# Squares of three row blocks on VectorE instead of ScalarE, and one row scaling in two pieces, in a single-core encoder layer

## The chip, the cores and the metric

The kernel runs on one core of a Trainium2 chip. The metric is the device time of one execution in microseconds. Each core has TensorE (matrix multiplications, here PE, its weight loads PEld), VectorE (DVE), ScalarE (ACT), GpSimd (POOL) and SyncE (SP), each with an instruction queue of its own that is worked off in order; here SyncE's queue issues the DMA transfers that move tiles between DRAM and the on-chip memories SBUF and PSUM.

## The reference

One layer of a bidirectional encoder over two sequences of 256 and 2048 tokens, each with the same 16 learned meta tokens in front, d_model = 1024. All arrays are float32. Cut to what matters:

```python
def hybrid_layer(z, norm_w, w_in, q_norm_w, k_norm_w, sink, conv_w, conv_b, ln_w, ln_b, w_out):
    h = rmsnorm(z, norm_w)                       # z * rsqrt(mean(z*z) + 1e-6) * norm_w, per token
    proj = jnp.einsum('bld,de->ble', h, w_in)    # 1024 -> 2816
    q, k, v, g_att, c_val, c_glu, g_conv = jnp.split(proj, SPLIT_IDX, axis=-1)
    q = rmsnorm(q.reshape(B, L, N_HEADS, HEAD_DIM), q_norm_w)
    k = rmsnorm(k.reshape(B, L, N_KV_HEADS, HEAD_DIM), k_norm_w)
    v = v.reshape(B, L, N_KV_HEADS, HEAD_DIM)
    att = windowed_gqa(q, k, v, sink).reshape(B, L, W_ATT) * jax.nn.silu(g_att)
    cnv = conformer_conv(c_val, c_glu, conv_w, conv_b, ln_w, ln_b) * jax.nn.silu(g_conv)
    mixed = jnp.concatenate([att, cnv], axis=-1)
    return z + jnp.einsum('ble,ed->bld', mixed, w_out)
```

The change is in the first line, the normalization: for each token the sum of the squares of its 1024 values, and the scaling by the inverse root of their mean.

## The kernel before

The 2320 tokens (16 meta tokens and 18 blocks of 128) are the columns of the input projection. They are cut into six groups: group 0 of 400 columns (the meta tokens and blocks 1 to 3 of the rows, in the code `SEGS0`), and groups 1 to 5 of 384 columns, three blocks each. Two chunks of three groups go through the projection, `CHUNKS`; a chunk goes through eleven units of 256 output columns of `w_in`, and an item is one unit for one group. A projected unit is accumulated in PSUM from 24 matmuls per half: each float32 operand is split into a high part `xh` (or `ws` high) in the fp32r format and the rest, `xl`, and for each of the eight slices of 128 input features three products are summed, high by high, high by `xl`, and low weight by `xh` (`proj_et`, matmuls at L831).

A row block is loaded by `stats(i)` from `z` into a tile `xn` (L693). The function that it returns, `rest`, sums the squares (L700, on ScalarE, with an accumulator) into `ssq`, and GpSimd computes 1/rms in two instructions, at L128 and L129, into column `i` of `rstd`. Index 0 is the meta tokens, 1 to 3 are the other blocks of group 0, 4 to 6 group 1, 7 to 9 group 2. Blocks 0 to 3 have tiles of their own and write their squares to a spare tile `sq0`; block 4 has a tile of another pool, blocks from 5 on share the two buffers of the tag `xn`, and their squares are written over the block. So the load of block 7 goes into the buffer of block 5, the load of 8 into that of 6, the load of 9 into that of 7.

Group 0 is normalized by rows: VectorE multiplies each block by its 1/rms (L1102), TensorE transposes it in eight pieces of 128 columns (`turn0`, L1074; six right away, two later), and `split0` makes `xh` on ScalarE (L1082) and `xl` on VectorE (L1084). In front of the transposes of each block stand some warm-up matmuls (`busy`, L1067; each float32 one is two instructions in the trace). The two first weight units are split by ScalarE (L806) and VectorE (L807); for the second of them VectorE and GpSimd take turns. The groups from 1 on are loaded already transposed (`zt`, L717). TensorE spreads the three columns of `rstd` over partitions by three transposes into `bc` (`Prep.first`, L729), VectorE scales (`Prep.scale`, L745), ScalarE casts to `xh` (L762), VectorE and GpSimd take turns at `xl` (`Prep.split`, L771). The first item's results are gated: a sigmoid on ScalarE gives `sg` (L874), for which another activation table is loaded, and VectorE multiplies into `us` (L886). The convolution on VectorE (L914) comes later, as do attention and output projection.

The program is written in an order of ticks (`later(k, f)` puts work off by k ticks). On each engine a scheduler then sets the order when the program is built, by a simulated timeline (the context is opened with `schedule_with_timeline_sim=True`): what is ready goes first, and among ready instructions that which was written first. An instruction wrapped in `pinned`, `tc.keep_in_program_order`, stays behind everything that was written ahead of it for its engine. Pinned here are the squares of blocks 0 to 6 and the splits of the first two weight units, the row scalings of group 0, the warm-ups and the first six transposes. The squares of blocks 7 to 9 and the transposes into `bc` are not. At the start of item 0 the second weight unit is split, and behind it the squares of group 1 are written; `Prep.first` of group 1 comes one tick into item 1, the loads of blocks 7 to 9 with it and their squares a tick later; `Prep.first` of group 2 comes one tick into item 2.

Of the kernel before, what the change touches and what calls it, by code (L numbers as in the profile page):

```python
# [14 lines left out]
AF = mybir.ActivationFunctionType  # L15
ALU = mybir.AluOpType
# [3 lines left out]
D = 1024  # L20
# [59 lines left out]
def hymba_kernel(  # L80
# [11 lines left out]
    nc = tc.nc  # L92
# [31 lines left out]
    rstd = const.tile([P, NB + 1], F32, name="rstd")  # L124

    def rsqrt(dst, src, scale, eps):
        n = src.shape[-1]
        nc.gpsimd.tensor_scalar(src, src, scale, eps, op0=ALU.mult, op1=ALU.add)  # L128
        nc.gpsimd.tensor_tensor(dst, src, half[: src.shape[0], 0:n], op=ALU.pow)  # L129
# [545 lines left out]
    if True:  # L675
        rows0 = {}
        sq0 = yp.tile([P, YW], F32, tag="y", name="sq0")

        def pinned(op, yes=True):
            if yes:  # L680
                tc.keep_in_program_order(op)

        def stats(i):
            rows = NM if i == 0 else P
            r0 = 0 if i == 0 else NM + P * (i - 1)
            if i < 4:
                xn = cp.tile([P, UWID], F32, tag="us", name=f"xn{i}")[:, :D]
                rows0[i] = xn
            elif i == 4:
                xn = yp.tile([P, YW], F32, tag="y", name=f"xn{i}")[:, :D]  # L690
            else:
                xn = sp.tile([P, D], F32, tag="xn", name=f"xn{i}")
            dma = nc.sync.dma_start(xn[:rows], z[r0 : r0 + rows, :])  # L693
            if i >= PIN_X:
                tc.keep_in_program_order(dma)

            def rest():
                ssq = sp.tile([P, 1], F32, tag="ssq", name=f"ssq{i}", bufs=4)
                sq = sq0[:, :D] if i < 4 else xn
                pinned(nc.scalar.activation(sq[:rows], xn[:rows], AF.Square, accum_out=ssq[:rows]), i < 7)  # L700
                rsqrt(rstd[:rows, i : i + 1], ssq[:rows], 1.0 / D, EPS)

            return rest
# [360 lines left out]
        def busy(pt, n):  # L1064

            for _ in range(n):
                tc.keep_in_program_order(nc.tensor.matmul(pt[:, :P], ident, ident, start=True, stop=True))  # L1067

        def turn0(i, d):

            o, rows = SEGS0[i]
            if d not in cols0:
                cols0[d] = psum.tile([P, 512], F32, tag="cdcdabcd"[d], name=f"xt0_{d}")
            return nc.tensor.transpose(  # L1074
                cols0[d][:, o : o + rows], rows0[i][:rows, P * d : P * d + P], ident[:rows, :rows]
            )
# [22 lines left out]
        for i in range(4):  # L1099
            r[i]()  # L1100
            o, rows = SEGS0[i]
            pinned(nc.vector.tensor_scalar(rows0[i][:rows], rows0[i][:rows], rstd[:rows, i : i + 1], None, op0=ALU.mult))  # L1102
            busy(warmup, (10, 5, 2, 3)[i])
            for d in range(6):
                tc.keep_in_program_order(turn0(i, d))
# [176 lines left out]
```

## Time and profile before

| what | value |
|---|---|
| median of three runs | 959.06 us (958.97 to 959.19) |
| profiled execution, its own time | 959.35 us |
| span of its trace | 957.6 us |
| TensorE busy | 948.4 us, 99% |
| VectorE busy | 754.3 us, 79% |
| ScalarE busy | 423.1 us, 44% |
| GpSimd busy | 334.7 us, 35% |
| DMA, mean over the span | 178 GB/s |

Busy times are sums over the instructions of an engine in the profiled execution; TensorE's ends are modelled, and its warm-up matmuls count as busy too. Times in the rows are in microseconds from the start of the span, unless marked ns. In a row of the timeline the first number is the start, the second the time from the start of the first to the end of the last of the xN instructions merged in it, and in brackets stands how long the engine had been idle and what ended that.

### The profile page before, as it was taken

The page shows a single profiled execution, that of the slowest core. Times are in us where ns is not written, and L with a number is a line of the kernel's source. Part 1 is how long each engine was busy: PE and PEld are TensorE (multiplying, and loading weights), DVE is VectorE, ACT ScalarE, POOL GpSimd, SP SyncE. Part 2 cuts the span into 40 slices and gives each one's busy share as a digit, 9 for nine tenths or more (in the row PEclk, how much of TensorE's full clock was granted, in tenths as well). Part 3 has the DMA queues.
Part 4 walks back from the last instruction along what each step waited for, and adds up shares of the span by engine and source line. Part 5 has one row for each costly group of instructions (what it writes and reads, how often), then busy time and mean ns, then how long its engine had stood idle before and what let it go on. Part 6 is the DMA issues. An engine that isn't in the chain of part 4 may idle for free. (4 is left out here: it accounts for less than half of the span.)

```text
span 957.6 us, 16432 instructions
## 1 busy us (share of the span) xinstructions
PE 948.4 (99%) x5813; PEld 891.9 (93%) x5813; DVE 754.3 (79%) x1282; ACT 423.1 (44%) x1159; POOL 334.7 (35%) x518
## 2 busy tenths in 40 slices
PE   9999999999999999999999999999999999999998
PEld 8999999999999999999999999888888888888887
DVE  5669999988977789999995665667777777777773
ACT  7531112343458740011112456556665666656661
POOL 4400000273569300000001454655454544545442
PEclk9999999999999999999999999999999999999999
DMA  8683345775656584233334587955454455544411
GB/s 310 198 310 112 132 174 181 259 288 173 213 158 193 194 306 144 89 121 130 138 136 142 185 284 246 385 155 168 153 178 130 132 171 155 175 128 139 132 55 66
DMA packets 121585, 170.88 MB, mean 178 GB/s; under 512 B 9984, under 2 KB 84112, under 8 KB 121504
## 3 DMA queue, kind: packets, MB, share of 16 engines
q1 hardware_dynamic: 121504, 169.84, 53.0%
q8 instruction: 46, 0.75, 0.3%
q14 instruction: 35, 0.29, 0.1%
HBM read 107.10 MB, written 62.70 MB: 177 GB/s over the span
## 5 line engine op out<-in xcount | busy, mean ns | idle before, releaser
L831 PE MATMUL pj<-xh,ws 128*128 128x384 f32 (+1 forms) x1536 | 395.9, 338 | 0.1
L914 DVE SCALAR_TENSOR_TENSOR y<-us,cw,y 128x1167 f32<-128x1167 f32 x240 | 329.0, 1428 | 0.4
L831 PEld LDWEIGHTS pj<-xh,ws 128*128 128x128 f32 x1536 | 280.0, 188 | 0.4 <-ACT xh L1082 0.4
L831 PE MATMUL pj<-xl,ws 128*128 128x384 f32 (+1 forms) x768 | 260.7, 340 | 0.6 <-POOL xl L771 0.6
L583 PE MATMUL y<-wo,rest 128*128 128x512 f32 (+1 forms) x672 | 173.7, 396 | 0.0
L847 PE MATMUL pj<-ws,xh 128*128 128x256 f32 (+1 forms) x880 | 164.7, 284 | 1.0 <-DVE kn L1003 1.0
L831 PEld LDWEIGHTS pj<-xl,ws 128*128 128x128 f32 x768 | 144.1, 188 | 1.0 <-POOL xl L771 0.9
L847 PEld LDWEIGHTS pj<-ws,xh 128*128 128x128 f32 (+1 forms) x880 | 136.2, 187 | 2.0 <-ACT sqq L948 1.2
L583 PEld LDWEIGHTS y<-wo,rest 128*128 128x128 f32 x672 | 116.6, 189 | 19.6
L847 PE MATMUL pj<-ws,xl 128*128 128x256 f32 (+1 forms) x440 | 124.1, 282 | 0.0
L416 ACT ACTIVATE sb<-sb,nm 128x304 f32<-128x304 f32 (+4 forms) x144 | 77.1, 535 | 63.6 <-DVE nm L404 60.9
L474 DVE TENSOR_TENSOR ptiles<-pT,ptiles 128x512 fp32r<-128x512 f32 x100 | 68.6, 686 | 31.3 <-ACT ptiles L473 30.5
L939 ACT ACTIVATE go<-pj 128x384 f32<-128x384 f32 x48 | 23.5, 491 | 154.4 <-PE pj L831 141.0
L404 DVE CUSTOM_DVE_ANT_0 sb<-S,bias,vec 128x304 f32<-128x304 f32 (+4 forms) x144 | 73.5, 512 | 20.6 <-PE S L349 17.7
L128 POOL TENSOR_SCALAR ssk<-ssk 128x2 f32<-128x2 f32 x18 | 9.1, 508 | 212.4 <-ACT sqk L953 210.5
L847 PEld LDWEIGHTS pj<-ws,xl 128*128 128x128 f32 (+1 forms) x440 | 82.2, 187 | 0.3
L439 POOL TENSOR_SCALAR sb<-sb,es 128x304 f32<-128x304 f32 (+4 forms) x144 | 71.9, 516 | 3.6
L473 ACT CAST ptiles<-pT 128x512 fp32r<-128x512 f32 x100 | 58.0, 581 | 31.6 <-PE pT L462 30.8
L128 POOL TENSOR_SCALAR ssq<-ssq 128x4 f32<-128x4 f32 (+2 forms) x55 | 28.4, 517 | 103.3 <-ACT xn L700 73.9
L349 PEld LDWEIGHTS S<-kw,q 128*128 128x128 f32 x288 | 52.8, 188 | 12.3 <-ACT ptiles L473 0.9
L497 PE MATMUL O<-ptiles,v 128*128 128x512 f32 x200 | 64.2, 402 | 0.0
L349 PE MATMUL S<-kw,q 128*128 128x304 f32 (+4 forms) x288 | 61.6, 297 | 0.8 <-issue 0.5
(127 smaller groups left out, 1264.3 us busy)
## 6 DMA issues: line engine op xcount, KB each, us to landing
wd<-ws SPq DMA_DIRECT2D x36, 512.0 KB, 5.7
ws<-wd SPq DMA_DIRECT2D x36, 512.0 KB, 5.9
wraw<-in_w_in SPq DMA_DIRECT2D x52, 256.0 KB, 5.8
xn<-in_z SPq DMA_DIRECT2D x18, 512.0 KB, 5.2
gd<-go SPq DMA_DIRECT2D x48, 192.0 KB, 2.0
yo<-in_z SPq DMA_DIRECT2D x36, 256.0 KB, 3.1
out_y<-yo SPq DMA_DIRECT2D x35, 256.0 KB, 2.1
kw<-kd SPq DMA_DIRECT2D x16, 512.0 KB, 5.3
```

Source lines behind the costliest of these rows:

```text
L128: nc.gpsimd.tensor_scalar(src, src, scale, eps, op0=ALU.mult, op1=ALU.add)
L349: r = f(*a, **k)
L404: nc.vector.tensor_tensor_reduce(out=sb[:, n, c0:c1], in0=ps[:, 0:w], in1=cst["bias"][:, kv, n, c0 - QB * n : c1 - QB * n], scale=1.0, sca ...
L416: nc.scalar.activation(sb[:, n, c0:c1], sb[:, n, c0:c1], AF.Exp, bias=nm[:, n : n + 1], scale=-1.0, accum_out=rs[:, n : n + 1],)
L439: nc.gpsimd.tensor_scalar(sb[:, k, a0:a1], sb[:, k, a0:a1], es[:, k : k + 1], 1.0, op0=ALU.mult, op1=ALU.mult)
L473: nc.scalar.copy(ph, pt)
L474: nc.vector.tensor_tensor(pl, pt, ph, op=ALU.subtract)
L497: nc.tensor.matmul(o, lhs, t, start=(start and i == 0), stop=(stop and i == 1))
L583: nc.tensor.matmul(ps, mh[mi][:, e % 4, :], wo[e, wi][:, cols], start=(e == 4 and k == 0), stop=(e == 3 and k == 2),)
L831: nc.tensor.matmul(ps[:, :n], ws[:, d, wi, P * half_i : P * half_i + P], x[xi][:, d, o : o + n], start=(k == 0), stop=(k == 3 * ND - 1),)
L847: nc.tensor.matmul(ps[:rows, :UW], x[xi][:, d, o : o + rows], ws[:, d, wi, :], start=(k == 0), stop=(k == 3 * ND - 1),)
L914: nc.vector.scalar_tensor_tensor(y[:, yo + o0 : yo + o1], u[:, o0 + k : o1 + k], cw[:, j, k : k + 1], y[:, yo + o0 : yo + o1], op0=ALU.mul ...
```

## The change

The squares of blocks 4 to 6, the second group of columns (group 1), are summed by VectorE with one `tensor_tensor_reduce` per block, which multiplies the block by itself, writes the products over it and sums them. They are pinned, as the activations were, now on VectorE's queue: behind the last split of the second weight unit. The pin of the other squares is kept for blocks 0 to 3. In the first group (group 0), the last block, number 3, is scaled in two instructions of 512 columns instead of one of 1024; the warm-ups and the transposes behind it stay as they are.

```diff
--- before.py
+++ after.py
@@ -697,7 +697,21 @@
             def rest():
                 ssq = sp.tile([P, 1], F32, tag="ssq", name=f"ssq{i}", bufs=4)
                 sq = sq0[:, :D] if i < 4 else xn
-                pinned(nc.scalar.activation(sq[:rows], xn[:rows], AF.Square, accum_out=ssq[:rows]), i < 7)
+                if 4 <= i < 7:
+                    pinned(
+                        nc.vector.tensor_tensor_reduce(
+                            out=xn[:rows],
+                            in0=xn[:rows],
+                            in1=xn[:rows],
+                            scale=1.0,
+                            scalar=0.0,
+                            op0=ALU.mult,
+                            op1=ALU.add,
+                            accum_out=ssq[:rows],
+                        )
+                    )
+                else:
+                    pinned(nc.scalar.activation(sq[:rows], xn[:rows], AF.Square, accum_out=ssq[:rows]), i < 4)
                 rsqrt(rstd[:rows, i : i + 1], ssq[:rows], 1.0 / D, EPS)
 
             return rest
@@ -1099,7 +1113,9 @@
         for i in range(4):
             r[i]()
             o, rows = SEGS0[i]
-            pinned(nc.vector.tensor_scalar(rows0[i][:rows], rows0[i][:rows], rstd[:rows, i : i + 1], None, op0=ALU.mult))
+            for a in (0, D // 2) if i == 3 else (0,):
+                part = rows0[i][:rows, a : a + D // 2] if i == 3 else rows0[i][:rows]
+                pinned(nc.vector.tensor_scalar(part, part, rstd[:rows, i : i + 1], None, op0=ALU.mult))
             busy(warmup, (10, 5, 2, 3)[i])
             for d in range(6):
                 tc.keep_in_program_order(turn0(i, d))
```

## Rows read from the trace of the kernel before

**Rows 1.** Page part 1: busy us, share of the span, instructions.

```profile
PE 948.4 (99%) x5813; PEld 891.9 (93%) x5813; DVE 754.3 (79%) x1282; ACT 423.1 (44%) x1159; POOL 334.7 (35%) x518
```

**Rows 2.** Windows by stretch; the last three: granted clock, DMA share, GB/s.

```profile
16.00:31.40 15.40, 15.40 (x87) 15.35 (x87) 10.18 (x18) 12.43 (x24) 7.07 (x13) 1.00 0.72 249
31.40:34.00 2.60, 2.04 (x12) 1.41 (x11) 2.60 (x8) 2.60 (x7) 2.52 (x4) 1.00 0.01 3
34.00:100.00 66.00, 66.00 (x372) 66.00 (x372) 51.89 (x63) 17.13 (x33) 10.45 (x10) 1.00 0.67 227
100.00:957.60 857.60, 850.99 (x5263) 796.89 (x5261) 681.93 (x1183) 379.80 (x1078) 309.86 (x475) 1.00 0.52 172
```

**Rows 3.** Timeline, 9.5 to 13 us: start, duration, engine, line.

```profile
10.29 0.75 PEld L1067 LDWEIGHTS warmup<-ident 128*128 128x128 f32 x6
10.34 0.75 DVE L1102 TENSOR_SCALAR xn<-xn,rstd 128x1024 f32<-128x1024 f32 x1 [0.71 <-POOL rstd L129]
...
11.14 0.64 PEld L1074 LDWEIGHTS xt<-ident,xn 128*128 128x128 f32 x6
...
11.51 1.08 ACT L1082 ACTIVATE xh<-xt,vec 128x400 fp32r<-128x400 f32 x2 [1.11 <-PE xt L1074]
12.14 1.18 DVE L1084 SCALAR_TENSOR_TENSOR xl<-xt,vec,xh 128x400 fp32r<-128x400 f32 x2 [0.45 <-ACT xh L1082]
```

**Rows 4.** VectorE's groups by line and shape: busy us, mean ns, idle before.

```profile
L914 DVE SCALAR_TENSOR_TENSOR y<-us,cw,y 128x1167 f32<-128x1167 f32 x240 | 329.0, 1428 | 0.4
...
L404 DVE CUSTOM_DVE_ANT_0 sb<-S,bias,vec 128x304 f32<-128x304 f32 x112 | 59.4, 530 | 10.9 <-PE S L349 8.4
L807 DVE TENSOR_TENSOR ws<-wraw,ws 128x512 fp32r<-128x512 f32 x50 | 34.7, 728 | 7.1 <-ACT ws L806 7.1
...
L404 DVE CUSTOM_DVE_ANT_0 sb<-S,bias,vec 128x176 f32<-128x176 f32 x8 | 3.2, 399 | 5.4 <-PE S L349 5.3
...
L1102 DVE TENSOR_SCALAR xn<-xn,rstd 128x1024 f32<-128x1024 f32 x3 | 2.3, 753 | 3.2 <-POOL rstd L129 3.2
...
L1120 DVE TENSOR_SCALAR vec<-vec 128x2 f32<-128x2 f32 x1 | 0.2, 169 | 2.3 <-DMA vec<-in_vecs 2.3
```

**Rows 5.** Timeline, 18 to 28 us, the second group's squares and its scaling.

```profile
18.16 3.01 POOL L807 TENSOR_TENSOR ws<-wraw,ws 128x512 fp32r<-128x512 f32 x2 [2.71 <-ACT ws L806]
...
18.29 3.43 DVE L807 TENSOR_TENSOR ws<-wraw,ws 128x512 fp32r<-128x512 f32 x2
...
18.96 1.11 ACT L700 ACTIVATE xn<-xn 128x1024 f32<-128x1024 f32 x1
...
22.26 1.28 ACT L874 ACT_TABLE_LOAD   x1
...
24.09 0.72 DVE L886 TENSOR_TENSOR us<-pj,sg 128x271 f32<-128x271 f32 x3 [2.38 <-ACT sg L874]
...
26.94 0.43 PEld L729 LDWEIGHTS bc<-ident,rstd 128*128 128x128 f32 x3
...
27.65 4.29 DVE L745 SCALAR_TENSOR_TENSOR xt<-xt,vec,bc 128x384 f32<-128x384 f32 x8 [2.84 <-PE bc L729]
```

**Rows 6.** Timeline, 18 to 35 us, blocks 7 to 9 and what stands behind.

```profile
21.23 5.54 SPq L693 DMA_DIRECT2D xn<-in_z  x3
...
30.09 1.06 ACT L700 ACTIVATE xn<-xn 128x1024 f32<-128x1024 f32 x1 [1.11 <-DMA xn<-in_z]
...
31.15 2.98 ACT L762 CAST xh<-xt 128x384 fp32r<-128x384 f32 x7
...
31.60 0.54 POOL L129 TENSOR_TENSOR rstd<-ssq,half 128x1 f32<-128x1 f32 x1
...
32.11 2.94 POOL L771 TENSOR_TENSOR xl<-xt,xh 128x384 fp32r<-128x384 f32 x2
...
32.21 0.31 PE L729 MATMUL bc<-ident,rstd 128*128 128x128 f32 x1
...
33.81 0.45 PE L831 MATMUL pj<-xl,ws 128*128 128x384 f32 x1 [0.56 <-POOL xl L771]
```

## The prediction

> **What bounds the kernel now.** I read the page first. TensorE is busy for 948.4 of 957.6 us [rows 1], so what can be won is 9.2 us, and what can be lost is any stretch in which TensorE is made to wait. The windows then say where the missing 9.2 us lie [rows 2]. Before 12.15 us TensorE fills its time with warm-up matmuls, so "busy" says little there: the first projection matmul waits for the first `xh`, at 12.15 (below). From 16.0 to 31.4 it is busy for 15.40 of 15.40, in 31.4 to 34 for 2.04 of 2.60, from 34 to 100 without a gap, and after 100 it idles 6.61 us in 857.6. Both halves of the change act ahead of 34 us. The question is therefore narrow: does the first projection matmul come earlier than 12.15, and does TensorE wait more or less than now around 26.9 (where it needs the second group's 1/rms) and 31.4 to 34 (where it starts on the second group's columns)? After that TensorE runs on without a gap for 66 us, so a microsecond gained or lost there is carried along; only the few waits behind 100 us could swallow part of it. [...]
>
> **Part one, the last block of rows in two halves.** Now VectorE scales the block in one instruction, 10.34 to 11.09, and TensorE's first weight load of that block starts at 11.14 [rows 3]. In front of those transposes stand six warm-up weight loads, which fill 10.29 to 11.04. So even if the first half were ready at once, the transposes could start at 11.04, not sooner: the gain is at most 0.10 us. The price of a half: 1024 columns take 753 ns and 2 columns 169 ns [rows 4], so 512 take (753+169)/2 = 461 ns by a straight line, and two of them 0.92 us, 0.17 more than now. The first half is ready at 10.34+0.46 = 10.80, before the warm-ups end; the second at 11.26, when TensorE is still at the first four blocks (six weight loads take 0.64, so four last until 11.04+0.43 = 11.47). The 0.17 us delays what is queued behind on VectorE, the weight split that now starts at 11.00; the next instruction that matters, the first `xl`, comes at 12.14 after 0.45 us of idle time spent on ScalarE's `xh`, and that covers it. Without this cover the part would cost 0.17 instead of gaining. ScalarE starts on `xh` at 11.51 as soon as the transposes let it. Value taken: minus 0.05 us, bounds minus 0.10 and plus 0.17.
>
> **Part two, what it removes.** Three squares leave ScalarE. In the trace they run without a gap from 18.96 until the table load for the sigmoid starts at 22.26, so 3.3 us [rows 5]. The table load, the first `sg` and with it the first `us` on VectorE (which waits 2.38 us for it, until 24.09) can start as much earlier. But TensorE does not wait for any of them: it is full from 16.0 to 31.4 [rows 2]. ScalarE's next work, the squares of blocks 7 to 9, waits for loads (1.11 us before the last of them, at 30.09 [rows 6]). So the freed time by itself is worth nothing at the end of the kernel.
>
> **What it adds.** Three multiply-and-sum instructions over 128x1024 in float32 on VectorE. This size is not in the trace; the same instruction is at L404: 304 columns in 530 ns, 176 in 399 [rows 4], so 1.023 ns a column and 219 ns fixed, and 1024 columns take 1.27 us. Its sources there are one in PSUM and one in bf16; with two float32 sources in SBUF the nearest row is the convolution's L914, 1167 columns in 1428 ns, which with the same slope gives 1.28. Three of them are 3.81 us, against 3.3 on ScalarE. They are kept behind VectorE's part of the second weight split, two instructions that take 3.43 us, from 18.29 to 21.72, beside 3.01 us of the same on GpSimd [rows 5]: 1.7 us each, where this form has a mean of 728 ns over the kernel [rows 4]. So the sums start at 21.72 and not at 18.96, and end at 25.53. The upper bound comes from the same stretched pair, 1.72 us for 512 columns, so 3.4 for 1024; I don't take it, since GpSimd's long instructions end at 21.17 and what it does until the end of the sums is one column wide. The lower bound is the 1.27.
>
> **First place where it can bite: 26.94.** From the end of a block's square to the end of its 1/rms GpSimd takes 0.99 us (block 9: square ends at 30.09+1.06 = 31.15, power at 31.60+0.54 = 32.14 [rows 6]). So the last of the three is ready at 25.53+0.99 = 26.5. TensorE loads them at 26.94 [rows 5], from its place in the order and not from a wait. There remain 0.4 us: no stall, and VectorE's scaling of the second group can begin at 27.65 as now. The first `us` moves from 24.09 to 25.53 and is over at 26.25; the sums and it fit into what are now 2.38 and 2.84 us of idle time on VectorE. That is the cover. At 1.4 us a sum instead of 1.27 the cover is used up, and every further 0.1 us costs TensorE 0.3.
>
> [...]
>
> **Second place: blocks 7 to 9.** This is the part that I fear. Their tiles share two buffers with blocks 5 and 6, so the load of block 7 is queued on SyncE until the square of block 5 has been taken. That is now at 21.23, and the three loads hold the queue for 5.54 us, the third one waiting in turn for the square of block 7 [rows 6]. With the sums on VectorE block 5 is done at 21.72+2x1.27 = 24.26: all three loads, their squares and the last 1/rms shift by 24.26-21.23 = 3.03 us, the last square from 30.09 to 33.1 and the last power's end from 32.14 to 35.2. In the order of before, two things stand behind them. On ScalarE, seven of the second group's eight `xh` casts come after that last square (from 31.15). On TensorE, the transpose of block 9's 1/rms stands at 32.21, in the middle of the second group's matmuls. If both orders stayed, TensorE would lose about 3 us. But these instructions are not pinned: the program writes the casts and the matmuls ahead of them, and the scheduler has put them in front only because it counted on them being ready. With the sums on VectorE they are ready later for the scheduler too, and it will put some or all of the casts and matmuls first. Then ScalarE casts while VectorE is still scaling (4.29 us from 27.65), GpSimd's first `xl` (now started at 32.11 behind the power, 1.47 us) can start sooner, and the 0.56 us for which TensorE waits for it at 33.81 can shrink. Bounds of this term: minus 0.56 and plus 3.0. I take plus 0.4, an order that is moved in part: one late cast is waited for, and most of the 0.56 goes.
>
> **Sum.** The profiled execution took 959.35 us, 957.6 of span and 1.75 around it, and is 0.29 above the median of 959.06. Against that: -0.05 (halves), 0 (squares off ScalarE, sums under cover), +0.4 (blocks 7 to 9). Profiled 959.7, median 959.4.
>
> **Rivals.** A change under 0.2% (1.9 us) is about what a measurement of this kernel can't tell from none.
>
> *Rival one, slower: block 9 holds TensorE.* The scheduler leaves block 9's transpose, or its square in front of the casts, about where it is. It decides if block 9's 1/rms, ready at 35.2, is queued ahead of matmuls that could run at 32.2. Then 3.0 us are lost, of which up to 0.56 takes the place of the present wait: plus 2.4 to 3.0, so 961.5 to 962.1. For it: the loads land later than the order of now assumes already (ScalarE sits idle 1.11 us with casts queued behind), and the scheduler need not know of the 1.7 us instructions beside GpSimd. Against it: any shift of readiness that it sees moves them the right way.
>
> *Rival two, slower: the sums take twice the time per column.* Each takes 0.22+2x1.05 = 2.31 us, three end at 28.65, the 1/rms is ready at 29.6 and TensorE waits from 26.94: plus 2.7, so 961.8. For it only that the trace has no accumulating row with two such sources; against it L914.
>
> *Rival three, faster by over 0.2%.* The 0.56 and 0.10 us are not enough; the new order would have to remove a further 1.3 of the 6.61 us that TensorE idles after 100, near 957. Nothing in the profile ties those to this change, except that the whole order is made anew.
>
> **Chances.** Forecast (within 1.9 us, either sign) 0.66; rival one 0.21, rival two 0.07; rival three 0.06. So faster 0.06, same 0.66, slower 0.28. The likeliest case alone reaches from -0.7 (minus 0.56, minus 0.10) to +1.6 (half of the 3.0 us): 958.3 to 960.7. To leave out no more than two in ten the range must take in most of rival one: 958.2 to 962.0.
>
> **What would show it.** Halves: two L1102 instructions near 0.46 us, first `xh` at 11.4 to 11.5. Sums: three VectorE instructions near 1.27 us between 21.7 and 25.6; at 2.3, rival two, with an idle TensorE before the load of 26.94. Blocks 7 to 9: the load of block 7 issued near 24.3 and the last square near 33; then the question is what stands behind it on ScalarE and what TensorE's idle time between 31 and 37 is: under 1.5 us for my forecast, 3 us for rival one. The table load near 19 confirms the removal. The prediction is wrong if the sums do not start at 21.7 but beside GpSimd's work, or if TensorE's idle time after 100 us changes by more than 1 us.

## The result and the profile after

The changed kernel takes 962.39 us in the median of seven runs (961.70 to 962.50), the kernel before, run beside it, 959.16 (958.81 to 959.68, seven runs). The ratio is 1.0032, 95% interval 1.0023 to 1.0041: slower by 3.2 us, where 959.4 was forecast, and 0.39 above the upper end of the range. The profiled execution took 962.39 too, with a span of 960.6 against 957.6. Two executions in the sets further down, one of 1330.71 us and one of 1562.00, were disturbed and are in no ratio.

TensorE's share of the page tells little, as before [rows 1]:

```profile
PE 949.7 (99%) x5813; PEld 893.2 (93%) x5813; DVE 758.1 (79%) x1289; ACT 420.4 (44%) x1153; POOL 335.9 (35%) x518
```

Its windows tell where the time went (columns as in [rows 2]: busy time of TensorE, its weight loads, VectorE, ScalarE, GpSimd, then granted clock, DMA share, GB/s):

```profile
16.00:31.40 15.40, 15.40 (x87) 15.30 (x87) 12.62 (x22) 7.78 (x15) 7.80 (x11) 1.00 0.70 241
31.40:34.00 2.60, 1.17 (x7) 0.54 (x5) 2.54 (x7) 1.74 (x5) 0.84 (x4) 1.00 0.10 38
34.00:36.00 2.00, 0.90 (x5) 0.58 (x5) 1.25 (x2) 2.00 (x6) 2.00 (x3) 1.00 0.00 0
36.00:40.00 4.00, 4.00 (x14) 4.00 (x15) 2.44 (x4) 0.70 (x3) 3.43 (x3) 0.57 0.63 164
36.50:39.50 3.00, 3.00 (x11) 3.00 (x10) 1.44 (x2) 0.02 (x1) 2.93 (x3) 0.50 0.68 161
100.00:960.60 860.60, 854.52 (x5283) 800.56 (x5281) 685.50 (x1187) 380.66 (x1079) 310.04 (x475) 1.00 0.52 173
```

The window from 36 to 40 in the kernel before:

```profile
36.00:40.00 4.00, 4.00 (x24) 4.00 (x24) 1.89 (x4) 1.12 (x3) 2.34 (x3) 1.00 0.88 277
```

There are three parts. Up to 31.4 us TensorE is full in both. Between 31.4 and 36 it idles 1.43 + 1.10 = 2.53 us, before 0.56: plus 1.97. Then, although it works without a gap, the granted clock falls to 0.50 from 36.5 to 39.5: between 36 and 40 it gets through 14 matmuls where it got through 24, and ten at 4.00/24 us each are, as an estimate, 1.67 us. After 100 it idles 6.08 us where it idled 6.61 [rows 2]: minus 0.53. Together plus 3.1, and the spans differ by 3.0.

The timeline shows what the 2.53 us wait for:

```profile
18.28 3.42 DVE L821 TENSOR_TENSOR ws<-wraw,ws 128x512 fp32r<-128x512 f32 x2
...
19.14 1.28 ACT L888 ACT_TABLE_LOAD   x1
...
21.63 1.21 DVE L702 CUSTOM_DVE_ANT_0 xn<-xn 128x1024 f32<-128x1024 f32 x1
...
22.77 1.21 DVE L702 CUSTOM_DVE_ANT_0 xn<-xn 128x1024 f32<-128x1024 f32 x1
...
22.93 1.10 POOL L128 TENSOR_SCALAR ssq<-ssq 128x1 f32<-128x1 f32 x1 [1.78 <-DVE ssq L702]
...
24.02 5.04 SPq L693 DMA_DIRECT2D xn<-in_z  x3
24.12 1.41 POOL L129 TENSOR_TENSOR rstd<-ssq,half 128x1 f32<-128x1 f32 x1
...
26.80 0.54 POOL L129 TENSOR_TENSOR rstd<-ssq,half 128x1 f32<-128x1 f32 x1
...
27.11 0.38 PE L743 MATMUL bc<-ident,rstd 128*128 128x128 f32 x2
...
28.24 0.27 PE L743 MATMUL bc<-ident,rstd 128*128 128x128 f32 x1
...
28.55 4.29 DVE L759 SCALAR_TENSOR_TENSOR xt<-xt,vec,bc 128x384 f32<-128x384 f32 x8 [2.78 <-PE bc L743]
...
31.13 0.50 ACT L776 CAST xh<-xt 128x384 fp32r<-128x384 f32 x1
...
32.18 0.32 PE L743 MATMUL bc<-ident,rstd 128*128 128x128 f32 x1 [0.45 <-POOL rstd L129]
...
32.26 0.77 PE L845 MATMUL pj<-xh,ws 128*128 128x384 f32 x3
32.48 1.06 ACT L714 ACTIVATE xn<-xn 128x1024 f32<-128x1024 f32 x1 [0.86 <-DMA xn<-in_z]
...
33.54 2.98 ACT L776 CAST xh<-xt 128x384 fp32r<-128x384 f32 x7
...
33.99 0.54 POOL L129 TENSOR_TENSOR rstd<-ssq,half 128x1 f32<-128x1 f32 x1
...
34.51 3.96 POOL L785 TENSOR_TENSOR xl<-xt,xh 128x384 fp32r<-128x384 f32 x3
...
34.59 0.32 PE L743 MATMUL bc<-ident,rstd 128*128 128x128 f32 x1 [1.56 <-POOL rstd L129]
...
35.95 0.45 PE L845 MATMUL pj<-xl,ws 128*128 128x384 f32 x1 [0.51 <-POOL xl L785]
```

Read it backwards from 35.95. The 0.51 us there are for GpSimd's first `xl`, which can't start before its last 1/rms is done (34.53) and ScalarE has cast. Block 9's transpose waits 1.56 us, until 34.59, for the same 1/rms; block 8's waits 0.45 at 32.18. Block 9's square ends at 33.54, because its load is the last of three that hold SyncE's queue from 24.02 on instead of 21.23 [rows 6]; and seven casts stand behind that square on ScalarE, as before. 0.45 + 1.56 + 0.51 is 2.52, the 2.53 us but for rounding.

The halves, at the other end, did nothing that counts: the two take 0.88 us where 0.92 was forecast, and the first `xh` at 11.51, where it was [rows 3].

```profile
10.47 0.88 DVE L1118 TENSOR_SCALAR xn<-xn,rstd 128x512 f32<-128x512 f32 x2 [0.71 <-POOL rstd L129]
...
11.51 1.08 ACT L1096 ACTIVATE xh<-xt,vec 128x400 fp32r<-128x400 f32 x2 [1.14 <-PE xt L1088]
```

### The profile page after: what moved, and what is told of

It is laid out like the page before. It is cut to its first block, busy times and chain, and to the rows that moved or that the text cites. A ratio compares the mean times of both kernels' runs of the same rounds, so it can differ in the third digit from the quotient of the medians.

```text
span 960.6 us, 16432 instructions
## 1 busy us (share of the span) xinstructions
PE 949.7 (99%) x5813; PEld 893.2 (93%) x5813; DVE 758.1 (79%) x1289; ACT 420.4 (44%) x1153; POOL 335.9 (35%) x518
## 4 chain that ended last, share of the span: by engine, by line
PE 92%; DVE 3%; POOL 1%; issue 1%; DMA 1%; ACT 1%; SPq 0%; POOLq 0%; ACTq 0%; DVEq 0%
PE pj L845 41%; PE y L583 20%; PE pj L861 14%; PE O L497 5%; PE pT L462 4%; PE S L349 4%; DMA xn<-in_z 1%; PE O L349 1%; PE qT L349 1%; PE lnu L220 1%; PE lnt L201 1%; PE pT_m L459 0%; DVE y L928 0%; PE kt L1028 0%; DVE ptiles L474 0%
## 5 line engine op out<-in xcount | busy, mean ns | idle before, releaser
L474 DVE TENSOR_TENSOR ptiles<-pT,ptiles 128x512 fp32r<-128x512 f32 x100 | 68.6, 686 | 31.4 <-ACT ptiles L473 30.7
L128 POOL TENSOR_SCALAR ssk<-ssk 128x2 f32<-128x2 f32 x18 | 10.4, 578 | 211.0 <-ACT sqk L967 209.7
L128 POOL TENSOR_SCALAR ssq<-ssq 128x4 f32<-128x4 f32 (+2 forms) x55 | 26.0, 473 | 105.0 <-ACT xn L714 76.2
```

The costliest lines, as they stand in the source:

```text
L474: nc.vector.tensor_tensor(pl, pt, ph, op=ALU.subtract)
```

## The experiments

**Theory A:** the loss is the wait for blocks 7 to 9, which come 2.8 us later, at queues whose order was kept. Which queue does the holding is split: A1, the last square holds both ScalarE's casts and TensorE's transpose, and each of the two is worth the whole stall; A2, the transpose alone. **Rival C:** the sums themselves, by what they do to GpSimd and to the scaling of the second group. **Theory D** is on the second half of the loss: the clock falls because TensorE stood idle before. Each run went beside the kernel before on the same chip, and the ratio is to that.

**The two parts apart.** First the halves alone, in the kernel before:

```diff
-            pinned(nc.vector.tensor_scalar(rows0[i][:rows], rows0[i][:rows], rstd[:rows, i : i + 1], None, op0=ALU.mult))
+            for a in (0, D // 2) if i == 3 else (0,):
+                part = rows0[i][:rows, a : a + D // 2] if i == 3 else rows0[i][:rows]
+                pinned(nc.vector.tensor_scalar(part, part, rstd[:rows, i : i + 1], None, op0=ALU.mult))
```

> The kernel before with the two halves alone; the squares stay on ScalarE. Theory A (the whole loss comes from the later squares of blocks 7 to 9): 958.9 to 959.5 us, the same as before; TensorE's idle time between 31.4 and 36 us stays near 0.56 us. Rival B (the halves delay the start and carry part of the loss): 960 us or more, with the first xh later than 11.51.

Then the sums alone, which is this edit undone in the changed kernel:

> The kernel before with the three sums on VectorE alone; the block is scaled in one piece. Theory A: all of the loss, 962.0 to 962.8 us, TensorE idle 2.5 us between 31.4 and 36 and its granted clock at 0.50 for some 3 us behind it. Rival B: clearly less than the changed kernel, 961.5 us or below.

The halves alone take 959.51 us beside 959.11, ratio 1.0002 (0.9994 to 1.0011): nothing. The sums alone take 962.47 beside 959.11, ratio 1.0036 (1.0022 to 1.0050): the whole loss, as A had it. Of its five runs, one, the profiled one, took 961.21 with a mean granted clock of 1.00; the other four took 962.45 to 963.00 with 0.998. So the clock doesn't fall in each execution of one program, and the executions in which it does are here 1.2 us or more longer. In the changed kernel the two of seven runs at 1.00 took 961.70 and 962.17, the others 962.06 to 962.50, which is less apart. Executions differ at their start as well: the first projection matmul comes at 12.11 us in the profiled execution of the halves and at 12.15 in that of the sums; of the kernels further down, the first sum starts at 21.56 in the order 5, 6, 4 and at 22.43 with the gap filled, where the changed kernel has 21.63. In the profiled run of the sums alone TensorE idles in 31.4 to 36 as long as in the changed kernel (2.56 us), and the clock is 1.00 behind it:

```profile
31.40:36.00 4.60, 2.04 (x11) 1.08 (x9) 3.62 (x9) 3.72 (x9) 2.75 (x5) 1.00 0.06 25
36.00:40.00 4.00, 3.85 (x22) 3.86 (x23) 2.40 (x4) 0.70 (x2) 3.62 (x4) 1.00 0.59 160
```

**Blocks 7 to 9 in buffers of their own,** so that their loads need not wait for the sums:

```diff
-            elif i == 4:
+            elif i == 4 or 7 <= i < 10:
                 xn = yp.tile([P, YW], F32, tag="y", name=f"xn{i}")[:, :D]
```

> The changed kernel, but blocks 7 to 9 are loaded into buffers of another tag (those of block 4 and of the second weight unit's raw parts), so that their loads no longer wait for the squares of blocks 5 and 6. Theory A: the loss goes, 959.0 to 960.0 us; the last square of the three is over before 27 us, TensorE idles under 1 us between 31.4 and 36 and its clock stays at 1.00. Rival C (the sums cost the time themselves, through the later 1/rms of group 1 and the later scaling): 961 us or more.

961.40 us, ratio 1.0025 (1.0016 to 1.0035): theory A's number is missed, and the time lies where rival C had it. The loads did start early (20.09), but the order was made anew with them:

```profile
25.11 1.06 ACT L714 ACTIVATE xn<-xn 128x1024 f32<-128x1024 f32 x1 [5.96 <-DMA xn<-in_z]
...
26.34 0.19 POOL L128 TENSOR_SCALAR ssq<-ssq 128x1 f32<-128x1 f32 x1 [5.16 <-ACT xn L714]
...
28.11 0.32 PE L743 MATMUL bc<-ident,rstd 128*128 128x128 f32 x1 [0.81 <-POOL rstd L129]
...
29.01 0.32 PE L743 MATMUL bc<-ident,rstd 128*128 128x128 f32 x1 [0.57 <-POOL rstd L129]
...
30.39 4.29 DVE L759 SCALAR_TENSOR_TENSOR xt<-xt,vec,bc 128x384 f32<-128x384 f32 x8 [1.57 <-PE bc L743]
...
35.73 0.45 PE L845 MATMUL pj<-xl,ws 128*128 128x384 f32 x1 [1.42 <-DVE xl L785]
```

Now block 7's square stands ahead of the table load on ScalarE and holds it until 26.27; on GpSimd block 7's 1/rms stands ahead of group 1's, and TensorE waits for those 1/rms at 28.11 and 29.01 and, with the scaling from 30.39, 1.42 us for an `xl` at 35.73. The waits moved to another queue held by a square that was too early in it. This tells that the order of the squares matters, but doesn't separate A from C.

**The squares of blocks 7 to 9 behind the casts.** In the changed kernel they are pinned, so that they keep their written place, which is behind group 1's casts:

```diff
-                    pinned(nc.scalar.activation(sq[:rows], xn[:rows], AF.Square, accum_out=ssq[:rows]), i < 4)
+                    pinned(nc.scalar.activation(sq[:rows], xn[:rows], AF.Square, accum_out=ssq[:rows]), i < 4 or 7 <= i < 10)
```

> The changed kernel with the squares of blocks 7 to 9 pinned on ScalarE behind the eight casts of the second group that are written ahead of them; the loads come as late as in the changed kernel. The transposes of their 1/rms fall behind some 24 more matmuls on TensorE by themselves. Theory A (late loads, felt only through what is queued behind the last square): the loss nearly goes, 959.3 to 960.2 us; what is left is a wait of about 0.9 us for the first xl, because the scaling starts at 28.5 instead of 27.65. Rival C (the sums on VectorE cost the time themselves): 961 us or more.

**Only the transposes behind the matmuls.** Group 2's three transposes into `bc` are pinned instead, which puts them behind group 1's first 24 matmuls; the squares stay where the scheduler puts them:

```diff
-                    nc.tensor.transpose(
-                        bc[:, o : o + rows], rstd[:rows, i : i + 1].to_broadcast([rows, P]), ident[:rows, :rows]
+                    pinned(
+                        nc.tensor.transpose(
+                            bc[:, o : o + rows], rstd[:rows, i : i + 1].to_broadcast([rows, P]), ident[:rows, :rows]
+                        ),
+                        g == 2,
                     )
```

> The changed kernel with the three transposes of blocks 7 to 9's 1/rms pinned on TensorE behind the 24 matmuls that are written ahead of them; ScalarE's order is left, with the last square in front of seven casts. Theory A1 (two things are held by the last square, the transpose on TensorE and the casts on ScalarE, each worth the whole stall): no gain, 961.8 to 962.6 us, and TensorE now waits some 2 us for GpSimd's first xl. Theory A2 (the transpose alone holds TensorE): 959.0 to 960.0 us.

With the squares behind: 959.79 us beside 959.03, ratio 1.0010 (1.0001 to 1.0019). Most of the loss is gone (the ratio was 1.0032), with the sums still on VectorE: A holds, and C falls for the greater part. This pin moves more than the squares: the transposes of group 2, with no pin of their own, run from 40.81 on, behind group 1's matmuls. With the transposes alone: 963.04, ratio 1.0037 (1.0025 to 1.0050), no gain, and 0.4 us above what A1 expected: A2 falls. The wait only moves to the `xl`s, 1.04 us at 33.21 for VectorE's and 1.42 at 35.74 for GpSimd's, whose casts still stand behind block 9's square:

```profile
32.27 1.06 ACT L714 ACTIVATE xn<-xn 128x1024 f32<-128x1024 f32 x1 [0.95 <-DMA xn<-in_z]
...
33.33 2.98 ACT L779 CAST xh<-xt 128x384 fp32r<-128x384 f32 x7
...
35.74 0.44 PE L848 MATMUL pj<-xl,ws 128*128 128x384 f32 x1 [1.42 <-POOL xl L788]
```

So with the transposes out of the way the casts, and GpSimd's `xl` behind the last 1/rms, still hold TensorE as long. Whether the transposes alone would, with the casts free, has no run of its own. What is left with the squares behind is a wait for VectorE's first `xl`, which comes after eight scalings that start at 28.57 instead of 27.65 [rows 5]; this part is rival C's:

```profile
28.57 4.29 DVE L759 SCALAR_TENSOR_TENSOR xt<-xt,vec,bc 128x384 f32<-128x384 f32 x8 [2.79 <-PE bc L743]
...
29.21 4.19 ACT L776 CAST xh<-xt 128x384 fp32r<-128x384 f32 x8 [1.39 <-DVE xt L759]
...
33.31 1.05 ACT L714 ACTIVATE xn<-xn 128x1024 f32<-128x1024 f32 x1
...
33.90 0.44 PE L845 MATMUL pj<-xl,ws 128*128 128x384 f32 x1 [1.73 <-DVE xl L785]
...
40.81 0.38 PE L743 MATMUL bc<-ident,rstd 128*128 128x128 f32 x2
```

**Both orders in the kernel before.** The same two pins, without the change:

> The kernel before (squares on ScalarE, one scaling of 1024) with the squares of blocks 7 to 9 and the transposes of their 1/rms pinned behind the casts and the matmuls written ahead of them. Theory A: TensorE's wait of 0.56 us at 33.8 goes, and the wait for block 9's transpose: 958.2 to 958.9 us. Rival (those waits are replaced by one for the first xl or by a later third group): 959.0 us or more.

959.38 us beside 959.03, ratio 1.0006 (0.9997 to 1.0015): no gain, A's number is missed and the rival is right. The wait of 0.56 us for GpSimd's `xl` [rows 6] gives way to one of 0.83, at 34.07, for VectorE's, again behind eight scalings.

**The sums in the order of blocks 5, 6, 4,** so that block 5's buffer comes free one sum earlier:

```diff
-                for k in (4, 5, 6):
+                for k in (5, 6, 4):
                     r[k]()
```

> The changed kernel with the sums in the order 5, 6, 4 instead of 4, 5, 6: block 4 has a buffer of its own, so the buffers that the loads of 7 to 9 wait for come free one sum, 1.15 us, sooner, while the last of group 1's 1/rms comes when it did. Theory A: the chain of loads, last square and first GpSimd xl moves by that 1.15 us: 960.6 to 961.4 us. Rival C: as the changed kernel, 962.0 to 962.6 us.

960.18 us, ratio 1.0012 (1.0003 to 1.0021): better than expected, and C, which had 962.0 or more, falls here too, the more so as the scaling starts even later, at 28.86. The loads are issued 1.20 us earlier, at 22.82; the transposes of blocks 8 and 9 wait no more, and what is left is 1.01 us for ScalarE's casts, all eight of which now stand behind block 9's square, with a clock of 1.00:

```profile
22.82 5.01 SPq L693 DMA_DIRECT2D xn<-in_z  x3
...
28.86 4.29 DVE L759 SCALAR_TENSOR_TENSOR xt<-xt,vec,bc 128x384 f32<-128x384 f32 x8 [3.15 <-PE bc L743]
...
32.23 3.39 ACT L776 CAST xh<-xt 128x384 fp32r<-128x384 f32 x8
...
32.78 0.79 PE L845 MATMUL pj<-xh,ws 128*128 128x384 f32 x3 [1.01 <-ACT xh L776]
```

**The gap filled.** In the changed kernel five matmuls of the identity, whose results nobody reads, are queued between the transposes of blocks 8 and 9, where TensorE waits 1.56 us:

```diff
+                for o, rows, i in segs[:-1]:
+                    last = spread_rstd(o, rows, i)
+                if g == 2:
+                    for _ in range(5):
+                        with tc.issue_after(last.ins):
+                            last = nc.tensor.matmul(bc[:, 384:512], ident, ident, start=True, stop=True)
+                with tc.issue_after(last.ins):
+                    spread_rstd(*segs[-1])
```

> The changed kernel with five matmuls on the identity (results unused, some 1.4 us) queued on TensorE between the transposes of block 8's and block 9's 1/rms, where TensorE waits anyhow. Theory D (part of the loss is not the wait but the granted clock at half behind it, which falls because TensorE stood idle): the waits' ends stay where they are, the granted clock stays at 1.00 in every run, 961.2 to 961.9 us. Rival E (the clock falls for another reason): 962.2 us or more and a stretch at 0.50 in most runs.

960.83 us, ratio 1.0022 (1.0013 to 1.0032). That is 1.8 over the kernel before beside it, where the changed kernel was 3.2 over, and less than the 961.2 to 961.9 expected; the intervals of the two ratios still overlap. The mean granted clock is 1.00 in each of the nine runs, where in the changed kernel it was in two of seven. No operand comes earlier by it: from block 8's transpose to block 9's it is 2.38 us (32.97 to 35.35), in the changed kernel 2.41 (32.18 to 34.59). In this execution the first sum starts at 22.43, 0.80 us later than in the changed kernel, and the rows behind it stand later by about that.

```profile
32.97 0.32 PE L743 MATMUL bc<-ident,rstd 128*128 128x128 f32 x1 [0.43 <-POOL rstd L129]
...
35.35 0.32 PE L743 MATMUL bc<-ident,rstd 128*128 128x128 f32 x1 [0.42 <-POOL rstd L129]
```

```profile
31.40:36.00 4.60, 3.75 (x25) 3.00 (x23) 3.91 (x10) 3.77 (x10) 2.17 (x5) 1.00 0.24 95
36.00:40.00 4.00, 3.49 (x21) 3.29 (x20) 2.30 (x2) 1.28 (x4) 4.00 (x4) 1.00 0.50 119
```

So D holds: TensorE is busy in the gap (3.75 of 4.60 us instead of 2.07), and the clock doesn't fall behind it.

**A better order, without and with the change.** To the two pins, group 1's scalings and VectorE's `xl`s are pinned too, so that VectorE takes them in the written order, the first `xl` after four scalings and not after eight:

```diff
-                        nc.vector.scalar_tensor_tensor(
-                            xt[:, dd, :n], xt[:, dd, :n], nw[:, d : d + 1], bc[:, :n], op0=ALU.mult, op1=ALU.mult
+                        pinned(
+                            nc.vector.scalar_tensor_tensor(
+                                xt[:, dd, :n], xt[:, dd, :n], nw[:, d : d + 1], bc[:, :n], op0=ALU.mult, op1=ALU.mult
+                            ),
+                            self.g == 1,
                         )
...
-                        eng.tensor_tensor(xl[:, d, :n], xt[:, dd, :n], xh[:, d, :n], op=ALU.subtract)
+                        pinned(
+                            eng.tensor_tensor(xl[:, d, :n], xt[:, dd, :n], xh[:, d, :n], op=ALU.subtract),
+                            self.g == 1 and not dd,
+                        )
```

> This is the kernel before with the squares of blocks 7 to 9 and group 2's spreading transposes in written order (as the run before it of this kind), and group 1's scalings and VectorE's share of its xl in written order too, so that the first xl stands behind two or four scalings and not behind eight. Theory A (TensorE's idle time between 31.4 and 36 us is set by what stands ahead of the first xl on VectorE, ScalarE and GpSimd): the 0.8 us for which TensorE waited for VectorE's xl goes, idle time in 31.4 to 36 below 0.3 us, 0.2 to 0.6 below the kernel before: 958.4 to 958.9. Rival (the idle time turns up at the next operand, or behind 100 us): 959.0 to 959.6.

> The same orders in the changed kernel: squares of blocks 7 to 9 behind the casts, group 2's transposes behind group 1's matmuls, group 1's scalings and VectorE's xl in turns. Theory A: the 1.7 us that TensorE waited for VectorE's xl when the squares alone were put behind the casts shrinks to under 0.8, since the scaling starts near 28.5 and the first xl can follow it after some 2.5 us; idle time in 31.4 to 36 below 1 us, no fall of the granted clock: 958.8 to 959.5. Rival (the transposes into bc at 28.2 are too late whatever stands behind): idle time stays near 1.7, 959.6 to 960.2.

Without the change, 957.92 us beside 959.31, ratio 0.9986 (0.9977 to 0.9995): faster than both kernels, and below what was expected. TensorE has no gap left between 31.4 and 36:

```profile
31.40:36.00 4.60, 4.60 (x28) 4.60 (x27) 4.21 (x9) 4.09 (x8) 3.16 (x5) 1.00 0.69 179
```

```profile
27.65 2.19 DVE L749 SCALAR_TENSOR_TENSOR xt<-xt,vec,bc 128x384 f32<-128x384 f32 x4 [2.84 <-PE bc L730]
...
29.76 1.09 DVE L778 TENSOR_TENSOR xl<-xt,xh 128x384 fp32r<-128x384 f32 x1
```

Of the 1.5 us between the spans (956.1 and 957.6) that is 0.56. Another 0.63 are idle time between 200 and 300 us, 0.40 instead of 1.03, far from the edit, in an order made anew; the rest wasn't located. With the change, 959.22 beside 959.31, ratio 1.0000 (0.9991 to 1.0009), as A had it: no idle time in 31.4 to 36 either, a mean clock of 1.00 in all eleven executions, and the loss is gone. But the rival has a part of it: the scaling still starts late, and a wait of 1.01 us has turned up at the next group's `xl`, at 51.39:

```profile
51.39 0.44 PE L854 MATMUL pj<-xl,ws 128*128 128x384 f32 x1 [1.01 <-DVE xl L792]
```

In the same order the kernel without the change is 1.3 us faster than the one with it. With the squares behind the casts in both, and the transposes pinned only in the kernel before, it was 0.4 us faster (959.38 and 959.79). So much of the cost stays with the sums when the order is mended, and that is rival C's share.

## Why the prediction was wrong

**What bounds the kernel** was read rightly: the first projection matmul stayed at 12.15, TensorE full to 31.4, and everything was decided between there and 36 us. The idle time after 100 us changed by 0.53, within the 1 us that was allowed for.

**Halves:** forecast minus 0.05; alone they measure nothing within about 0.1%. The first `xh` is where it was.

**Squares off ScalarE** at nothing: right. The table load is at 19.14, and TensorE gained nothing from it.

**The sums:** they start at 21.63, as forecast, and take 1.21 us (forecast 1.27). They end at 25.13. Rival two, which had 2.31 us for each, falls. No run shows the doubled time per column that its sum was worked out with: the trace has 1.21 us for 1024 columns, under the name `CUSTOM_DVE_ANT_0`, with both float32 sources in SBUF.

**First place, 26.94:** no stall, as forecast, but the cover was thinner than worked out, and "VectorE's scaling of the second group can begin at 27.65 as now" failed. Block 6's 1/rms is ready at 26.80 + 0.54 = 27.34 and not at 26.5, since GpSimd's two small instructions for block 4 took 1.10 and 1.41 us beside the sums, where block 5's took 0.19 and 0.55 (below). That was not what counted, though: the third transpose stood later among the matmuls than before, and runs at 28.24 from its place in the order, 0.9 us after its operand. The scaling starts 0.90 us later. Where the casts are not held, this shows as a wait of 1.73 us at VectorE's first `xl`; in the changed kernel it lies under the longer wait for block 9.

**Second place, blocks 7 to 9:** this is the step that failed. The shift itself was right (load forecast for 24.26, issued at 24.02; last square 33.1, now 32.48; last 1/rms 35.2, now 34.53). Wrong was "it will put some or all of the casts and matmuls first", and with it the plus 0.4 for "an order that is moved in part". The scheduler moved no cast: the same one in front of block 9's square, the same seven behind. On TensorE the same three matmuls, and no more, stand between the transposes of blocks 8 and 9. In the kernel before, these two rows stood at

```profile
28.48 0.50 ACT L762 CAST xh<-xt 128x384 fp32r<-128x384 f32 x1
...
31.60 0.77 PE L831 MATMUL pj<-xh,ws 128*128 128x384 f32 x3
```

and in the changed kernel they stand at 31.13 and 32.26. That is rival one, to which 0.21 was given. Its price, 2.4 to 3.0, was for the wait, and the term taken was plus 0.4; it measured plus 1.97. The two pins show that TensorE is held by more than the transposes: with these alone behind the matmuls nothing is gained, with the squares behind the casts, where the transposes fall back as well, most of the loss goes.

**What no step had** is the clock. It is 1.00 in each window of the kernel before [rows 2], in an execution in which TensorE idled 0.56 us between 31.4 and 36. With 2.53 us idle there it fell to 0.50 in the profiled execution of the changed kernel, for some 1.67 us more by the estimate above. That takes this execution beyond the range: without it the sum is 959.35 + 1.97 - 0.53 = 960.8, inside, and the kernel with the gap filled took 960.83. It need not be all: of the changed kernel's two executions at a mean clock of 1.00 one, at 961.70, lies inside the range and one, at 962.17, still above it.

Why the scheduler kept the order was not tried; that its simulated timeline has the sums or the loads earlier than the chip does is only argued.

## What to carry to other kernels

When work moves to another engine, follow the buffers it frees: here three sums that took 3.5 us in place of 3.3 gave a buffer back 2.8 us later, and what that delayed stood in front of other work on two queues. An order made by a scheduler is no proof against that; if the cost of a change hangs on "the scheduler will move it", price the order that stays, and pin the late instruction behind the work that TensorE needs. Look at the granted clock behind a new gap of TensorE as well: here it fell to 0.50 for 3.0 us behind 2.53 us of idle time, and its mean was 0.998 in five of seven executions; with five queued matmuls that nobody reads it was 1.00 in nine of nine, at no cost that these runs show.

## What was not expected of the hardware

**GpSimd beside VectorE's sums.** The instruction at L128 on a column of 128x1, 0.19 us for the next two blocks, took 1.10 for block 4, beside the second sum, and ended at 24.03, 0.05 after it; that at L129, 0.54 to 0.55 for the next two, took 1.41 and ended at 25.53, 0.40 after the third. So each seems to have waited for the sum that was running. With the squares behind the casts, with the order 5, 6, 4 and with the gap filled, GpSimd's two instructions for the block summed first took 1.10 and 1.41 to 1.42 us too, and ended 0.05 after the second sum and 0.40 to 0.41 after the third. What holds them isn't shown.

**The granted clock** fell to 0.50 for 3.0 us after TensorE had taken up full work again, behind a stretch in which its longest single wait was 1.56 us. It did not do so in every execution. The kernel with the sums alone idled as long (2.56 us) in its profiled execution and kept 1.00, at 961.21 us against 962.45 and more for its others; the one with the transposes pinned had 1.00 from 36 to 40 after 2.51 us idle, at 961.64 against 963.04 and more. What decides between the two isn't shown.
